# A fourth pair of chunks in the second feed-forward, with one split made by ScalarE and an on-chip transfer

## The chip, the cores and the metric

The kernel runs on one core of one Trainium2 chip. The core has a matrix engine (TensorE, PE in the profile; its weight loads are listed apart as PEld), VectorE (DVE), ScalarE (ACT), GpSimd (POOL) and a sync engine (SP), which run side by side, each through its own queue of instructions in a fixed order. They wait for each other by semaphores. Transfers between the chip's memory and the on-chip buffer are issued from the queues of SP, ACT or POOL and are carried out by the core's 16 DMA engines. The metric is the device time of one execution in microseconds (us), as the median of several runs.

## What is computed

One block of a streaming encoder for 256 tokens of width 1024: a gated feed-forward, a mixing stage with two attention-like branches, a cross-attention to a memory of 256 rows, and a second gated feed-forward. The change is made in the code of the feed-forwards:

```python
def rmsnorm(x, g):
    x32 = x.astype(jnp.float32)
    y = x32 * lax.rsqrt(jnp.mean(x32 * x32, axis=-1, keepdims=True) + EPS)
    return (y * g.astype(jnp.float32)).astype(x.dtype)

def swiglu(h, w_in, w_down):
    gate, up = jnp.split(h @ w_in, 2, axis=-1)
    return (jax.nn.silu(gate) * up) @ w_down
...
        h = rmsnorm(x, ffn2_pre_g[l])
        x = x + 0.5 * rmsnorm(swiglu(h, ffn2_w_in[l], ffn2_w_down[l]), ffn2_post_g[l])
```

`w_in` is 1024 x 5632 (gate and up), `w_down` is 2816 x 1024; all data are 32-bit floats.

## The kernel before

**Two halves of every number.** TensorE multiplies a shortened float format (fp32r in the profile). To keep the accuracy of 32-bit floats, every matrix is split into `hi`, the value rounded to that format, and `lo`, the remainder. A product is then three matmuls: hi by hi, hi by lo and lo by hi. For weights, each tile of 128 x 1024 numbers (512 KB) is loaded into a `raw` buffer, ScalarE casts it to `hi` (line 153 for plain weights, 173 for tiles of pairs) and VectorE subtracts `hi` from it to get `lo` (lines 155 and 174). There are 4 `raw` buffers, 8 `hi` and 8 `lo` buffers.

**The feed-forward** (function `ffn`). The 2816 hidden columns are cut into 11 chunks of 256, and each chunk has 256 gate columns and 256 up columns, four weight tiles in all. A plain chunk (`act_tok`) is computed for both halves of 128 tokens, 24 matmuls of 128 x 512 for each. Then silu(gate) times up (`act_evac`, lines 450 to 455) gives the chunk's activation `at`; four transposes on TensorE and a split (`flush`, line 445) turn it into the left operand `act` of the second matrix. A down step (`down`) multiplies the activation of one chunk and one half of the tokens with two tiles of `w_down`, 12 matmuls, and adds it up in PSUM (`acc`). The last three chunks' down steps (`STAG = 3`) are left for a tail, ordered by halves of the output columns, because the last norm (`post`) can begin on a half when it is complete.

**Pairs** (function `act_pair`). Two neighbouring chunks c and c+1 can be computed together by a scheme of Strassen and Winograd's kind: the two chunks, the two halves of the tokens and the two halves of the 1024 input rows form a 2 x 2 by 2 x 2 product of blocks, which needs 7 block products instead of 8. A block product is 12 matmuls (function `product`). With Bkn for rows' half k and chunk (n = 1 is c, n = 0 is c+1), the right operands are, in the order of the products:

1. `sums` = B00, into bank b1, saved by ScalarE (line 613)
2. `sums` + `both` (B01), into bank b4, saved (line 622)
3. that plus B11, added to b1, saved (line 627)
4. B11 itself, added to b4, which gives chunk c for the first tokens (line 634)
5. `both` + B11, added to b1, saved (line 637), which gives chunk c for the second tokens (line 640)
6. B10, into bank b0, which gives chunk c+1 for the first tokens (line 652)
7. the sum of all, added to b1, which gives chunk c+1 for the second tokens

The left operands are the matching sums of the input's blocks; they are made once (`pair_inputs`, lines 537 to 544). Each right operand is two tiles, so a pair splits 14 tiles. The sums of blocks are made in place by VectorE (`add`, line 592), 8 tiles a pair. Where a pair is listed in `FETCHED`, `both` + B11 is not added by VectorE but by a second, accumulating load of B11 from the chip's memory, issued from POOL (line 565); that is 2 adds fewer. `sums` and `both` of a pair live in four buffers (`extra`, named sraw in the profile), and the next pair's loads go into them when they are free (`pair_loads`, line 563).

Between the products, `step_between` puts half a down step of an earlier chunk (12 matmuls) onto TensorE, as many as there are in the list handed over; what is left follows after the seventh product.

Before, the second feed-forward takes chunks 0, 1, 2, 5 and 8 in the plain way and (3,4), (6,7), (9,10) as pairs, with 6, 6 and 2 halves of down steps inside the pairs, and nothing is fetched twice; the first feed-forward has the pairs (4,5), (6,7), (9,10), all in `FETCHED`.

**What sets the order.** Within an engine, instructions stay in a fixed order, which a planner makes when the kernel is built. It takes the instructions in the order of the program as their priority and lets a later one go ahead when its inputs and a buffer are ready earlier by the planner's own costs. `tc.high_priority()` and `tc.issue_after(...)` bend that order by hand. On the chip the order is kept, and an instruction that waits holds up all that stand behind it on its engine.

Of the kernel before, what the change touches and what calls it, by code (L numbers as in the profile page):

```python
# [11 lines left out]
F32 = mybir.dt.float32  # L12
# [20 lines left out]

STAG = 3

TOKS = {"f1_in": (3, 8), "f2_in": (2, 5, 8)}

PAIRS = {"f1_in": (4, 6, 9), "f2_in": (3, 6, 9)}

L_ACT = 21  # L40
L_F1 = 24
# [11 lines left out]
M_T = (106, 119)  # L53
M_O = (136, 140)

FETCHED = {"f1_in": (4,6,9), "f2_in": ()}
R_AT = (66, 130, 188, 252, 286, 332)

FG = 3
# [26 lines left out]
def block_kernel(ctx: ExitStack, tc: tile.TileContext, wts, head_in, gf_in, x_in, mem_in, memT_in, cols, rows, fbias, masks, out):  # L86
# [54 lines left out]
    def parts_of():  # L141
        return [wp.tile([P, D], F32R, tag=t, name=nm(t), bufs=8) for t in ("hi", "lo")]

    def load_split(src, n=512, behind=None, parts=None):

        raw = wp.tile([P, D], F32, tag="raw", name=nm("raw"), bufs=4)
        hi, lo = parts or parts_of()
        r, h, l = raw, hi, lo
        if n < 512:
            r, h, l = (p.rearrange("p (k n) -> p k n", k=2)[:, :, :n] for p in (raw, hi, lo))  # L150
        loads.append(nc.sync.dma_start(r, src).ins)
        with tc.issue_after(behind[0]) if behind else nullcontext():
            casts.append(S.copy(h, r).ins)  # L153
        with tc.issue_after(behind[1]) if behind else nullcontext():
            los.append(V.tensor_tensor(out=l, in0=r, in1=h.bitcast(F32), op=ALU.subtract).ins)  # L155
        return hi, lo

    def unit(name, i):
        u = _AT[name] + i
        if u not in cache:  # L160
            cache[u] = load_split(wts[u - 4], behind=hold.get(u), parts=place.get(u))
        return cache[u]

    def chunk(name, c):
# [4 lines left out]
        o = (kb % 2) * 512  # L169
        return hi[:, o : o + n], lo[:, o : o + n]  # L170

    def split(hi, lo, src):
        a = S.copy(hi, src)  # L173
        b = V.tensor_tensor(out=lo, in0=src, in1=hi.bitcast(F32), op=ALU.subtract)  # L174
        return a.ins, b.ins

# [250 lines left out]
    def ffn(w_in, w_dn, X, r2, n_tok, i_row, first_half, second_half=None):  # L427
# [132 lines left out]
        def more(r, c, k, n, j, op):  # L560
            src = wts[_AT[w_in] + 4 * (c + 1 - n) + 2 * k + j - 4]
            if op is None:
                loads.append(nc.sync.dma_start(r, src).ins)
            else:
                G.dma_start(r, src, accum_op=op)

        def act_pair(c, between):
            sx, q = pairs_in

            def of(n):  # L570
                return lambda kk: (sx[n][:, 0, kk], sx[n][:, 1, kk])

            def of_x(k):
                return lambda kk: (X.hi(4 * k + kk, 0, P), X.lo(4 * k + kk, 0, P))

            def splits(t):
                u = []
                for r in t:
                    p = parts_of()
                    split(p[0], p[1], r)  # L580
                    u.append(p)
                return u

            def raws(k, n):
                t = [wp.tile([P, D], F32, tag="raw", name=nm("raw"), bufs=4) for _ in range(2)]
                for j in range(2):
                    more(t[j], c, k, n, j, None)
                return t

            def add(t, o):  # L590
                for x, y in zip(t, o):
                    V.tensor_tensor(out=x, in0=x, in1=y, op=ALU.add)  # L592
# [12 lines left out]
            def half_tile(n):  # L605
                return sp.tile([P, 512], F32, tag="z2", name=nm(n), bufs=3)

            sums, both = sums_of_pair.pop(c)
            copies = [m4([P, 2, 512], n=n) for n in ("vw", "pc")]
            p1, v, w, p5 = (t[:, i] for t in copies for i in range(2))  # L610
            b1 = mm()
            product(b1, of_x(0), splits(sums), True)
            S.copy(p1, b1)
            add(sums, both)
            if c in FETCHED[w_in]:
                for j in range(2):
                    more(both[j], c, 1, 1, j, ALU.add)
            for _ in range(2 if c == 3 else 1):
                step_between()
            b4 = mm()  # L620
            product(b4, of("de"), splits(sums), True)
            S.copy(p5, b4)
            step_between()
            raw = raws(1, 1)
            add(sums, raw)
            product(b1, of("aed"), splits(sums), False)
            S.copy(v, b1)
            step_between()
            product(b4, of("baed"), splits(raw), False)
            if c not in FETCHED[w_in]:  # L630
                add(both, raw)
            with tc.high_priority():
                t = half_tile("c01")
                V.tensor_tensor(out=t, in0=b4, in1=v, op=ALU.subtract)
# [64 lines left out]
        for c in range(n_tok, NFF):  # L699
# [51 lines left out]
            while done < (NFF - STAG if last == NFF - 1 else min(c - 1 - (c + 1 in pairs), NFF - STAG - 1)):  # L751
# [856 lines left out]
```

## Time and profile before

| | |
|---|---|
| median of 3 runs | 772.19 us (772.18 to 773.46) |
| profiled execution | 772.46 us, of which 770.6 us are the span of the trace |
| PE busy | 762.0 us (99%) |
| VectorE busy | 635.2 us (82%) |
| ScalarE busy | 505.3 us (66%) |
| POOL busy | 20.4 us (3%) |
| DMA, hardware queue of SP | 144.83 MB, 53.9% of the 16 engines' span |
| DMA, POOL's queue | 4.60 MB, 3.1% |
| granted TensorE clock | 0.999 |

The profile is one execution. Busy times are sums over the span and hide that stages differ; a row of a stretch gives them for a part of it. Rows of groups have the form: line, engine, operation, what it writes and reads, shapes, count, then busy time and mean duration in ns, then idle time of the engine just before and who ended it. The chain of waits follows the last instruction back to what released it, step by step; what stands in it set the end, what doesn't was hidden. Rows of the timeline and of the chain begin with the start and the length in us. A matmul's row is longer than the distance to the next one, as they overlap; twelve in a row show the pace.

The second feed-forward begins at about 585 us; its first pair's inputs are made around 622 to 633 us, its pairs run until about 742 us, and its tail from there to 764 us.

### The profile page before, as it was taken

The numbers are of one execution on the slowest core, as the hardware profiler recorded it, in microseconds if no ns is written. First come the engines' busy times: TensorE is split into PE (matmuls) and PEld (weight loads), VectorE is DVE, ScalarE is ACT, GpSimd is POOL, SyncE is SP. The second block draws the span as 40 slices with busy tenths as digits, with TensorE's granted clock in tenths as the row PEclk, the third lists the DMA queues.
The fourth block names the chain that finished last, engine by engine and source line by source line (L and its number), as shares of the span: only waits on it lengthen the run. The fifth ranks groups of instructions, "written<-read, shape, count | busy, mean of one in ns | idle before, by whom it ended". The sixth has DMA issues, their size and how long they took to land.

```text
span 770.6 us, 11688 instructions
## 1 busy us (share of the span) xinstructions
PE 762.0 (99%) x4326; PEld 646.7 (84%) x4326; DVE 635.2 (82%) x939; ACT 505.3 (66%) x816; POOL 20.4 (3%) x42
## 2 busy tenths in 40 slices
PE   9999999999999999999999999999999999999996
PEld 8888788888888998898888888889888888888885
DVE  6799998998778898887776665885679899999973
ACT  8667576688774659667686345862668567775762
POOL 0000000000000100200000000000000000000000
PEclk9999999999999999999999999999999999999999
DMA  9768767674744545736476654466075616558331
GB/s 346 242 250 243 223 226 281 184 247 161 238 151 147 185 139 195 272 124 210 136 271 222 219 173 159 161 197 213 30 255 178 241 65 232 205 195 307 100 135 55
DMA packets 45129, 150.54 MB, mean 195 GB/s; under 512 B 5160, under 2 KB 8880, under 8 KB 45072
## 3 DMA queue, kind: packets, MB, share of 16 engines
q1 hardware_dynamic: 43168, 144.83, 53.9%
q0 software_dynamic: 1472, 4.60, 3.1%
q8 instruction: 34, 0.56, 0.3%
q10 hardware_dynamic: 432, 0.37, 0.1%
q14 instruction: 23, 0.19, 0.1%
HBM read 148.72 MB, written 1.06 MB: 194 GB/s over the span
## 4 chain that ended last, share of the span: by engine, by line
PE 90%; DVE 6%; DMA 2%; issue 1%; ACT 1%; DVEq 0%; ACTq 0%; SPq 0%
PE mm L100 46%; PE acc L100 36%; PE tr L100 5%; DVE sraw L592 1%; DVE lo L155 1%; DVE lo L174 1%; PE tr L445 1%; PE tr L385 1%; DMA sraw<-in_wts_dram 1%; DMA raw<-in_wts_dram 1%; DMA head<-in_head_dram 0%; DVE sx L174 0%; PE tr L1245 0%; ACT hi L153 0%; PE tr L1339 0%
## 5 line engine op out<-in xcount | busy, mean ns | idle before, releaser
L155 DVE TENSOR_TENSOR lo<-raw,hi 128x1024 fp32r<-128x1024 f32 (+1 forms) x204 | 241.3, 1200 | 37.5 <-ACT hi L153 30.9
L153 ACT CAST hi<-raw 128x1024 fp32r<-128x1024 f32 (+1 forms) x204 | 207.1, 1034 | 58.8 <-PE mm L100 30.4
L100 PE MATMUL mm<-hi,hlT 128*128 128x512 f32 (+1 forms) x688 | 209.4, 382 | 0.0
L100 PEld LDWEIGHTS mm<-hi,hlT 128*128 128x128 f32 x688 | 127.2, 188 | 22.3
L100 PE MATMUL mm<-lo,hlT 128*128 128x512 f32 (+1 forms) x344 | 130.1, 382 | 0.0
L100 PE MATMUL acc<-hi,act 128*128 128x512 f32 x352 | 113.6, 390 | 0.0
L173 ACT CAST hi<-sraw 128x1024 fp32r<-128x1024 f32 x60 | 62.6, 1052 | 25.5 <-DVE sraw L592 15.8
L100 PE MATMUL mm<-hi,sx 128*128 128x512 f32 x240 | 77.8, 390 | 0.0
L100 PEld LDWEIGHTS acc<-hi,act 128*128 128x128 f32 x352 | 66.1, 188 | 13.4
L100 PEld LDWEIGHTS mm<-lo,hlT 128*128 128x128 f32 x344 | 64.6, 188 | 10.8
L174 DVE TENSOR_TENSOR lo<-sraw,hi 128x1024 fp32r<-128x1024 f32 x60 | 72.1, 1220 | 0.8 <-ACT hi L173 0.5
L100 PE MATMUL acc<-lo,act 128*128 128x512 f32 x176 | 69.3, 394 | 0.0
L100 PE MATMUL acc<-hlT,hi 128*128 128x512 f32 x256 | 64.4, 393 | 0.0
L100 PEld LDWEIGHTS acc<-hlT,hi 128*128 128x128 f32 x256 | 46.1, 189 | 8.3
L100 PEld LDWEIGHTS mm<-hi,sx 128*128 128x128 f32 x240 | 44.9, 188 | 9.3
L100 PE MATMUL mm<-lo,sx 128*128 128x512 f32 x120 | 46.9, 391 | 0.1
L100 PEld LDWEIGHTS acc<-lo,act 128*128 128x128 f32 x176 | 33.1, 188 | 6.5
L100 PEld LDWEIGHTS acc<-hlT,lo 128*128 128x128 f32 x256 | 35.0, 190 | 2.5
L592 DVE TENSOR_TENSOR sraw<-sraw,raw 128x1024 f32<-128x1024 f32 x30 | 36.0, 1220 | 0.7 <-DMA raw<-in_wts_dram 0.6
L100 PE MATMUL acc<-hlT,lo 128*128 128x256 f32 x256 | 36.2, 283 | 0.0
L174 DVE TENSOR_TENSOR lo<-raw,hi 128x1024 fp32r<-128x1024 f32 x24 | 28.8, 1219 | 0.8 <-ACT hi L173 0.8
L100 PEld LDWEIGHTS mm<-lo,sx 128*128 128x128 f32 x120 | 22.5, 188 | 5.2 <-DVE lo L174 0.5
(285 smaller groups left out, 1192.4 us busy)
## 6 DMA issues: line engine op xcount, KB each, us to landing
raw<-in_wts_dram SPq DMA_DIRECT2D x223, 512.0 KB, 4.4
sraw<-in_wts_dram SPq DMA_DIRECT2D x24, 512.0 KB, 6.5
raw<-in_gf_dram SPq DMA_DIRECT2D x12, 344.0 KB, 3.8
sraw<-in_wts_dram POOLq DMA_DIRECT2D x6, 512.0 KB, 6.7
head<-in_head_dram SPq DMA_DIRECT2D x7, 392.0 KB, 6.3
grow<-in_rows_dram SPq DMA_DIRECT2D x4, 512.0 KB, 5.8
xs<-in_x_dram SPq DMA_DIRECT2D x2, 512.0 KB, 7.4
cb<-cd POOLq DMA_DIRECT2D x2, 512.0 KB, 6.1
```

Of the source, the lines that this page charges most:

```text
L100: log.append(PE.matmul(*args, **kw).ins)
L153: casts.append(S.copy(h, r).ins)
L155: los.append(V.tensor_tensor(out=l, in0=r, in1=h.bitcast(F32), op=ALU.subtract).ins)
L173: a = S.copy(hi, src)
L174: b = V.tensor_tensor(out=lo, in0=src, in1=hi.bitcast(F32), op=ALU.subtract)
L385: PE.transpose(blocks[-1][1], src(kb), ident)
L445: PE.transpose(trv[:, j, h * P : (h + 1) * P], ats[c, h][:, j * P : (j + 1) * P], ident)
L592: V.tensor_tensor(out=x, in0=x, in1=y, op=ALU.add)
```

## The change

- In the second feed-forward, chunks 5 and 8 are no longer plain: the pairs become (3,4), (5,6), (7,8), (9,10). The plain chunks are 0, 1 and 2.
- For the pairs 5, 7 and 9, `both` + B11 is made by the accumulating load (`FETCHED`), for pair 3 still by VectorE.
- For all four pairs, `lo` of B11 is made in another way (`BY_DMA`, `lo_by_dma`): ScalarE writes -1 times the raw tile, rounded to the format of `lo`, into `lo`, and a transfer from on-chip buffer to on-chip buffer, issued from POOL, adds the raw tile to it. `hi` is cast as before.
- In both feed-forwards, the two splits of B11 are called earlier: ahead of the sum for the third product instead of after the step that follows the third product.
- The down steps inside the second feed-forward's pairs are at most those of two chunks (4 halves): 0 and 1 in pair 3, 2 and 3 in pair 5, 4 and 5 in pair 7, 6 and 7 in pair 9. In the last pair, the step between the fifth and sixth product is left out, so its last half goes ahead of the seventh.
- Activations that have not been transposed by the end of the loop are flushed ahead of the tail.
- `TOTAL` is an option that is empty in both feed-forwards, and no B10 is in `BY_DMA`.

```diff
-TOKS = {"f1_in": (3, 8), "f2_in": (2, 5, 8)}
-
-PAIRS = {"f1_in": (4, 6, 9), "f2_in": (3, 6, 9)}
+TOKS = {"f1_in": (3,8), "f2_in": (2,)}
+
+PAIRS = {"f1_in": (4,6,9), "f2_in": (3, 5, 7, 9)}
...
-FETCHED = {"f1_in": (4,6,9), "f2_in": ()}
+TOTAL = {"f1_in": (), "f2_in": ()}
+FETCHED = {"f1_in": (4,6,9), "f2_in": (5, 7, 9)}
+
+BY_DMA = {("f2_in", c, "b11") for c in (3, 5, 7, 9)}
...
+    def lo_by_dma(l, r):
+        S.mul(l, r, -1.0)
+        G.dma_start(l.bitcast(F32), r, accum_op=ALU.add)
+
...
-    def split(hi, lo, src):
+    def split(hi, lo, src, by_dma=False):
         a = S.copy(hi, src)
+        if by_dma:
+            return lo_by_dma(lo, src)
         b = V.tensor_tensor(out=lo, in0=src, in1=hi.bitcast(F32), op=ALU.subtract)
...
             raw = raws(1, 1)
+            u11 = splits(raw, "b11")
             add(sums, raw)
             product(b1, of("aed"), splits(sums), False)
+            if c in TOTAL[w_in]:
+                for j in range(2):
+                    more(sums[j], c, 1, 0, j, ALU.add)
             S.copy(v, b1)
             step_between()
-            product(b4, of("baed"), splits(raw), False)
+            product(b4, of("baed"), u11, False)
...
-            step_between()
+            if c + 1 < NFF - 1 or first_half:
+                step_between()
             b0 = trp()
             raw = raws(1, 0)
             m = len(log)
-            product(b0, of_x(1), splits(raw), True)
+            product(b0, of_x(1), splits(raw, "b10"), True)
             if late[:1] == [c]:
                 flush(m + 10)
-            add(sums, raw)
+            if c not in TOTAL[w_in]:
+                add(sums, raw)
...
-                downs = [(i, h) for i in range(done, min(c, NFF - STAG - 1)) for h in range(2)]
-                done = max(done, min(c, NFF - STAG - 1))
+                upto = max(done, min(c, NFF - STAG - 1) if first_half else min(c, done + 2, NFF - STAG))
+                downs = [(i, h) for i in range(done, upto) for h in range(2)]
+                done = upto
...
+        while late:
+            flush(len(log))
         left, right = (0, 512), (512, 1024)
```

More of the change, by code (lines that the diff above doesn't have):

```diff
@@ L142, in parts_of, with load_split @@
         return [wp.tile([P, D], F32R, tag=t, name=nm(t), bufs=8) for t in ("hi", "lo")]
-    def load_split(src, n=512, behind=None, parts=None):
+    def lo_by_dma(l, r):
+        S.mul(l, r, -1.0)
+        G.dma_start(l.bitcast(F32), r, accum_op=ALU.add)
+    def load_split(src, n=512, behind=None, parts=None, by_dma=False):
         raw = wp.tile([P, D], F32, tag="raw", name=nm("raw"), bufs=4)
@@ L153, in load_split @@
             casts.append(S.copy(h, r).ins)
+        if by_dma:
+            lo_by_dma(l, r)
+            return hi, lo
         with tc.issue_after(behind[1]) if behind else nullcontext():
@@ L160, in unit @@
         if u not in cache:
-            cache[u] = load_split(wts[u - 4], behind=hold.get(u), parts=place.get(u))
+            cache[u] = load_split(wts[u - 4], behind=hold.get(u), parts=place.get(u), by_dma=(name, i) in BY_DMA)
         return cache[u]
@@ L170, in blk @@
         return hi[:, o : o + n], lo[:, o : o + n]
-    def split(hi, lo, src):
+    def split(hi, lo, src, by_dma=False):
         a = S.copy(hi, src)
+        if by_dma:
+            return lo_by_dma(lo, src)
         b = V.tensor_tensor(out=lo, in0=src, in1=hi.bitcast(F32), op=ALU.subtract)
@@ L574, in of_x, with splits @@
                 return lambda kk: (X.hi(4 * k + kk, 0, P), X.lo(4 * k + kk, 0, P))
-            def splits(t):
+            def splits(t, of=None):
                 u = []
@@ L579, in splits @@
                     p = parts_of()
-                    split(p[0], p[1], r)
+                    split(p[0], p[1], r, (w_in, c, of) in BY_DMA)
                     u.append(p)
```

## The prediction

> **What bounds the kernel now.** I read the page first, then the busy times by stretch, then the chain of waits, then the groups and single rows of the second feed-forward. The page says that TensorE is busy all the time and carries nine tenths of the chain.
>
> ```profile
> span 770.6 us, 11688 instructions
> ...
> PE 762.0 (99%) x4326; PEld 646.7 (84%) x4326; DVE 635.2 (82%) x939; ACT 505.3 (66%) x816; POOL 20.4 (3%) x42
> ...
> PE 90%; DVE 6%; DMA 2%; issue 1%; ACT 1%; DVEq 0%; ACTq 0%; SPq 0%
> ```
>
> Those shares are means over unlike stages. The stretches tell more (columns: length, then busy time of PE, PEld, DVE, ACT, POOL, then granted clock, DMA share, GB/s). The first runs from the first down step inside the first pair of the second feed-forward to the start of its tail, the second covers the three pairs of the first feed-forward.
>
> ```profile
> 622.70:747.70 125.00, 124.84 (x566) 102.53 (x565) 121.24 (x131) 86.38 (x108) 0.00 (x0) 1.00 0.54 190
> ...
> 40.00:165.00 125.00, 124.05 (x565) 102.16 (x564) 119.45 (x131) 87.23 (x111) 5.24 (x6) 1.00 0.71 231
> ```
>
> In the stretch that the change rewrites, PE idles 0.16 us of 125, at full clock; VectorE works 121.24 us and so has only 3.76 us to spare. Both are at their limit. The chain shows how close the second one is:
>
> ```profile
> 612.37 4.22 DMA raw<-in_wts_dram
> ...
> 633.50 1.06 ACT hi L173
> ...
> 655.76 2.35 DVE lo L155 x2
> 658.12 0.41 DVE at L455
> ...
> 658.57 0.44 PE tr L445 x2
> 659.01 12.28 PE mm L100 x54
> 671.28 2.72 PE acc L100 x12
> ...
> 685.38 5.44 PE mm L100 x24
> ...
> 741.71 2.75 PE acc L100 x12
> 744.45 0.43 PE tr L445 x4
> 744.89 19.08 PE acc L100 x84
> ```
>
> Up to 658.57 us the chain runs through VectorE (the `lo` and `at` rows): in the first pair, VectorE sets the pace. From there to 763.97 it is TensorE alone. Twelve matmuls, which are one product or one half of a down step, take 2.72 us; two `lo` in a row take 2.35 us, so one takes 1.13 us of VectorE when they follow each other.
>
> **The change part by part.**
>
> *Fourth pair.* Chunks 5 and 8 leave the plain path and the pairs become (3,4), (5,6), (7,8), (9,10). Two plain chunks are 96 matmuls, a pair is 7 x 12 = 84. The down steps, their weights and the transposes stay the same in number. So PE loses 12 matmuls: -2.72 us, and since PE idles only 0.16 us in the stretch, this is on the path.
>
> *VectorE's bill.* These groups are those of the stretch 622.7 to 747.7, the last one ScalarE's of 598.6 to 750:
>
> ```profile
> L155 DVE TENSOR_TENSOR lo<-raw,hi 128x1024 fp32r<-128x1024 f32 x27 | 32.3, 1220 | 1.7 <-ACT hi L153 1.6
> ...
> L592 DVE TENSOR_TENSOR sraw<-sraw,raw 128x1024 f32<-128x1024 f32 x16 | 19.3, 1219 | 0.0
> L174 DVE TENSOR_TENSOR lo<-raw,hi 128x1024 fp32r<-128x1024 f32 x12 | 14.4, 1218 | 0.0
> ...
> L634 DVE TENSOR_TENSOR c<-mm,vw 128x512 f32<-128x512 f32 x3 | 2.1, 685 | 0.0
> ...
> L173 ACT CAST hi<-raw 128x1024 fp32r<-128x1024 f32 x12 | 12.4, 1050 | 1.9 <-DMA raw<-in_wts_dram 0.9 <-ACT hi L153 0.7 <-ACT hi L173 0.4
> ```
>
> Before, the pairs and plain chunks 5 and 8 need 3 x 14 + 8 = 50 `lo`; after, 4 x 14 less the 8 of B11 make 48. Adds: 3 x 8 = 24 before; after 8 in pair 3 and 6 in the three pairs whose `both` is fetched, 26. These cancel. The fourth pair adds three combining subtractions or additions (lines 634, 640, 652), 3 x 0.6 = 1.8 us. So VectorE needs 121.24 + 1.8 = 123.0 us, and PE leaves it 125.0 - 2.72 = 122.3 us: the by-transfer `lo` and the fetched sums do not relieve VectorE, they only pay for the fourth pair. There is one cushion. VectorE's last piece, the `lo` of the last activation, ends at 747.7 (the row of 747.01 below) while its down step comes after twelve matmuls of the tail. The last 84 matmuls are one half step of chunk 7 and the tail's six groups, so the tail starts at 744.89 + 2.7 = 747.6 and that step at 750.3. That leaves 2.6 us: VectorE has 122.3 + 2.6 = 124.9 us for 123.0 us of work and may idle 1.9 us before PE pays. It idled 3.76 us before. If it idles as much again, 1.9 us of the gain are given back; if it idles little, because a queue that is behind does not wait, nothing. I take 0.7, nearer to nothing: 1.7 us of the idle time stand in the L155 row, as waits for casts of plain chunks and down weights, and the plain chunks go. Ends: 0 and 1.9.
>
> *ScalarE.* 6 more casts (56 against 42 + 8) and 8 multiplications by -1, which the trace doesn't show; by the cast of the same shape 1.05 us each. 14 x 1.05 = 14.7 us on 86.38 of 122.3 us: hidden, if the order on its queue is good.
>
> *B11's lo by transfer.* The new chain is cast, multiplication, issue on POOL, accumulating transfer. The nearest rows are the first feed-forward's accumulating loads:
>
> ```profile
> L565 POOL DMA_DIRECT2D sraw<-in_wts_dram x6: 853/868/916, 54.9 to 133.7; - x6
> ...
> DMA to landing us min/median/max: 5.1/6.7/8.3
> ```
>
> From the start of the cast to the landing: 1.05 + 1.05 + 0.87 + 6.7 = 9.7 us (8.1 to 11.3). The second tile's casts come 2.1 us later, and its first use is six matmuls (1.36 us) later. What is available is seen from when B11 is cast now and when its product starts (pair 3, 6 and 9; the product of pair 6 is the chain's 685.38):
>
> ```profile
> 634.46 2.00 ACT L173 CAST hi<-raw 128x1024 fp32r<-128x1024 f32 x2
> 675.44 1.06 ACT L173 CAST hi<-raw 128x1024 fp32r<-128x1024 f32 x1 [0.69 <-ACT hi L153]
> 720.73 2.00 ACT L173 CAST hi<-raw 128x1024 fp32r<-128x1024 f32 x2
> ...
> 639.95 0.39 PE L100 MATMUL mm<-hi,sx 128*128 128x512 f32 x1
> ...
> 727.58 8.18 PE mm L100 x36
> ```
>
> 5.5 us, 9.9 us and 9.6 us (730.3 - 720.7). With the old order pair 3 would come 4.2 us late. But the change calls this split ahead of the sum for the product before it, and the raw tile of pair 3 has landed by 616.6 (the chain's 612.37 + 4.22), so it can start as soon as the first product gives its buffers back, six steps of 2.72 us (16 us) ahead of the fourth product. In the later pairs it is five steps, 13.6 us. I take no stall; ends 0 and 4.2 us a pair. Queued behind on POOL is only the other tile's transfer and the fetched `both`, whose product is one step later.
>
> The Trainium skill, page "DMA: Bandwidth & Descriptors", section "Anatomy of one DMA — SWDGE (gpsimd) path", gives 2.0 us plus bytes over 436 KB per us for such a transfer, an estimate of 3.2 us for 512 KB. By it the chain from the cast would be about 6.2 us, the forecast the same 770.2 us and the late transfer no rival in pairs 6 and 9; the row of 6.7 us is of the same kind of transfer and decides.
>
> *Pairs without a plain chunk between.* The next pair's tiles can only be loaded when this pair's last split has freed theirs. The first feed-forward has one such place (pair 4 to 6), on the chain:
>
> ```profile
> 84.46 5.61 DMA sraw<-in_wts_dram
> ...
> 90.16 1.23 DVE sraw L592
> 91.39 1.14 DVE lo L155
> 92.52 0.41 DVE at L455
> ...
> 92.97 0.44 PE tr L445 x2
> ```
>
> The load is released late, the add waits for it at the head of VectorE's queue, `at` waits behind, and PE waits about 1 us. After the change there are three such places, with no down step after the last product; but each pair has 2 x 1.13 us less to do on VectorE than that one. I count the wait into the 0.7 above; ends 0 and 3 x 1 = 3 us.
>
> *Tail and flush.* The last pair now uses its four down steps inside (one is skipped), so nothing covers the last activation but the tail's first twelve matmuls.
>
> ```profile
> 742.91 0.46 ACT L450 ACTIVATE sg<-mm,facs 128x256 f32<-128x256 f32 x1
> ...
> 744.80 1.04 ACT L153 CAST hi<-raw 128x1024 fp32r<-128x1024 f32 x1
> ...
> 747.01 0.68 DVE L174 TENSOR_TENSOR act<-tr,act 128x512 fp32r<-128x512 f32 x1
> ```
>
> From the silu's start to the end of the activation's `lo` 4.8 us pass now, with a down weight's cast of 1.04 us within; twelve matmuls and four transposes are 2.72 + 0.43 = 3.1 us. Ends 0 and 1.7 us; I take 0, as that cast can come earlier when the down steps do, and matmuls of the other half of the columns are ready to fill the hole.
>
> *First feed-forward.* B11's split moves ahead there too, with `lo` still on VectorE: 2.3 us more before the third product's `lo`. In pair 6 these end at 101.5 and the product starts at 104.8, a lead of 3.3 us, so it is covered. Ends -1 (the wait above goes by chance of the new order) and +1 us.
>
> ```profile
> 99.17 2.36 DVE L174 TENSOR_TENSOR lo<-sraw,hi 128x1024 fp32r<-128x1024 f32 x2
> ...
> 104.78 2.72 PE mm L100 x12
> ```
>
> Sum: -2.72 + 0.7 = -2.0 us on the profiled execution of 772.46 us (span 770.6 and 1.9 around it). That execution lies 0.27 us above the median of the runs, so 772.19 - 2.0 = 770.2 us.
>
> **The rivals.**
>
> *Given back, no change.* VectorE idles as before, or the three joints cost 1 us each: 772.2 - 2.7 + 1.9 to 3.0 = 771.4 to 772.5 us. For it: VectorE's 123.0 against 122.3 us. Against it: the second half of the stretch is PE alone on the chain.
>
> *Slower: B11's lo lands late.* Place: the fourth product of each pair. It decides from 2.72 / 4 = 0.7 us a pair on. If the casts stay where they stand now, pair 3 costs 4.2 us and the others about 0.3 each: +2.4, 774.6 us; with 2 us in each pair +5.3, 777.5 us. For it: queue orders are fixed ahead and pair 6 has no slack at all. Against it: the new place of the split.
>
> *The transfers crowd the loads.* Eight transfers on chip and six fetched sums are 14 x 0.52 = 7.3 MB.
>
> ```profile
> q0 software_dynamic: 1472, 4.60, 3.1%
> ```
>
> At this queue's rate (3.1% of 770.6 us for 4.6 MB, 5.2 us a MB) they take 38 us, and the DMA share goes from 0.54 to (67.5 + 38) / 122.3 = 0.86. The first feed-forward runs at 0.71 with the 1 us above. If a load lands 1.5 us later at each of three joints, and PE pays that beside the 1 us, 3 x 2.5 = 7.5: +4.8, 777.0 us. The page "DMA: Bandwidth & Descriptors" of the Trainium skill says under "Issuing engines are not separate DMA queues" that all issuers share the same 16 engines, which is the mechanism of this rival; the shares here fit it.
>
> **How the numbers follow.** Forecast (give-back under 1.2 us): 0.45, with its own range 769.0 to 770.7. Given back: 0.30. Late lo: 0.17. Crowded loads: 0.08. A measurement of this kernel tells about 0.2%, 1.5 us, from no change; so faster 0.45, same 0.30, slower 0.25. Low end: the full 2.72, PE's 0.16 us of idle time in the stretch and a third of the first feed-forward's possible 1 us, 769.0. High end: into the late-lo case, past 774.6, to 775.0, which leaves out about 0.1 above.
>
> **What would show it.** Right: PE's busy time in the stretch about 2.7 us shorter, 12 matmuls fewer, VectorE near 100% busy from 620 to 745, the tail's row unchanged, POOL with eight more transfers landing in 5 to 8 us before the fourth product. Wrong: waits of PE on an accumulating transfer (late lo), on `at` or on sraw loads at 650, 680 and 710 (joints), landing times of loads up (crowding), or new gaps between 55 and 165 us (first feed-forward).

## The result, and the profile after

The changed kernel takes 778.75 us (median of 4 runs, 778.34 to 779.33) against 772.18 us before: a ratio of 1.0082 (95% interval 1.0064 to 1.0099). It is slower by 6.6 us, where 770.2 us and a range up to 775.0 us were forecast. The profiled execution of the changed kernel is one of 779.33 us, with a span of 777.5 us. Its page:

```profile
span 777.5 us, 11754 instructions
...
PE 761.3 (98%) x4314; PEld 645.3 (83%) x4314; DVE 636.5 (82%) x942; ACT 518.5 (67%) x834; POOL 33.7 (4%) x56
...
q1 hardware_dynamic: 43168, 144.83, 53.4%
q0 software_dynamic: 3488, 11.94, 7.9%
...
PE 71%; DVE 12%; DMA 9%; issue 5%; ACT 2%; POOL 0%; SPq 0%; DVEq 0%; ACTq 0%; POOLq 0%
```

The twelve matmuls are gone (4314 against 4326), but only 71% of the chain is TensorE's (90% before), and 9% is now DMA. The stretches say where; the columns are as in the prediction, the first row is of the kernel before, the two below of the changed one:

```profile
622.00:750.00 128.00, 127.84 (x580) 105.02 (x580) 121.94 (x132) 86.38 (x108) 0.00 (x0) 1.00 0.53 185
```

```profile
622.00:750.00 128.00, 119.35 (x532) 97.21 (x531) 116.94 (x126) 94.50 (x119) 12.20 (x14) 0.99 0.81 240
...
40.00:165.00 125.00, 124.89 (x568) 102.88 (x567) 120.29 (x133) 87.36 (x112) 5.19 (x6) 1.00 0.73 235
```

The first feed-forward has gained (TensorE idles 0.11 us of 125 instead of 0.95). In the pairs of the second one TensorE idles 8.65 us of 128, and VectorE, which the prediction put at its limit, idles 11 us. Both wait for something else. TensorE's waits from 600 us on:

```profile
PE tr L457 <- DVE at L467: 5.1, 2, 2.8
PE tr L457 <- DVE at L465: 3.2, 1, 3.2
```

These are three waits of 2.8, 2.3 and 3.2 us, each at the transposes of an activation (line 457, `flush`) in the midst of the sixth product, in the pairs 5, 7 and 9: 8.3 us. VectorE delivers `at` late. What made VectorE late in the pair 5 is read backwards, from VectorE's rows to ScalarE's to the loads (SP) and the transfers (the chain):

```profile
669.09 1.23 DVE L186 TENSOR_TENSOR lo<-raw,hi 128x1024 fp32r<-128x1024 f32 x1 [1.94 <-ACT hi L183]
672.59 1.23 DVE L186 TENSOR_TENSOR lo<-raw,hi 128x1024 fp32r<-128x1024 f32 x1 [2.27 <-ACT hi L183]
...
680.94 0.48 DVE L467 SCALAR_TENSOR_TENSOR at<-c,q,sg 128x256 f32<-128x256 f32 x1
```

```profile
668.01 1.05 ACT L183 CAST hi<-raw 128x1024 fp32r<-128x1024 f32 x1 [2.27 <-DMA raw<-in_wts_dram]
671.51 1.05 ACT L183 CAST hi<-raw 128x1024 fp32r<-128x1024 f32 x1 [2.45 <-DMA raw<-in_wts_dram]
```

```profile
663.75 2.81 SPq L575 DMA_DIRECT2D raw<-in_wts_dram  x2
```

```profile
656.11 0.09 POOL lo L149
656.19 1.09 issue
657.28 8.83 DMA lo<-raw
...
666.23 5.20 DMA raw<-in_wts_dram
671.43 0.02 issue
...
671.51 1.06 ACT hi L183
...
672.59 1.23 DVE lo L186
```

B10, the operand of the sixth product, is loaded late: its second load is issued at 666.2, the moment the on-chip transfer of B11's second tile lands, because that transfer reads the `raw` buffer which B10's load wants. It lands at 671.4. VectorE, with B10's two `lo` ahead of everything else in its fixed order, stands still for 1.94 and 2.27 us and starts `at` at 680.94. And the transfer itself took 8.8 us. The stretches show the engines of the DMA at that time (columns as above, the last two are DMA share and GB/s; the first is when the two fetches of `both` run, the second when the two transfers on chip run, the third has plain loads only):

```profile
651.00:656.50 5.50, 5.50 (x25) 4.53 (x25) 5.50 (x8) 5.50 (x8) 1.27 (x2) 1.00 0.99 186
660.00:664.50 4.50, 4.50 (x24) 3.70 (x22) 4.29 (x5) 4.50 (x6) 0.00 (x0) 1.00 1.07 221
672.00:674.00 2.00, 2.00 (x10) 1.67 (x9) 1.41 (x2) 0.56 (x1) 0.00 (x0) 1.00 1.01 401
```

All 16 engines are busy in all three, but the accumulating transfers move 186 and 221 KB per us (GB/s in the rows) and the plain loads 401. A pair with fetches and transfers on chip so keeps the engines busy for some 10 us with 2 MB, and all that comes in between waits: two loads of down weights, issued at 654, move from 657 to 661, and the transfers on chip, issued at 656.1 and 657.3, move from 660 on.

Two ways are left in which this makes B10 late. **Hold**: the transfer keeps the raw buffer until it lands, so the load is issued late. **Queue**: the packets of plain loads stand behind the accumulating ones, so the transfers and the loads themselves take longer. The experiments are to tell them apart, and both from the prediction's bound, **VectorE's amount of work**.

### The profile page after: what moved, and what is told of

The parts are those of the page before. It is cut to its first block, busy times and chain, and to the rows that moved or that the text cites. A ratio compares the mean times of both kernels' runs of the same rounds, so it can differ in the third digit from the quotient of the medians.

```text
span 777.5 us, 11754 instructions
## 1 busy us (share of the span) xinstructions
PE 761.3 (98%) x4314; PEld 645.3 (83%) x4314; DVE 636.5 (82%) x942; ACT 518.5 (67%) x834; POOL 33.7 (4%) x56
## 3 DMA queue, kind: packets, MB, share of 16 engines
q1 hardware_dynamic: 43168, 144.83, 53.4%
## 4 chain that ended last, share of the span: by engine, by line
PE 71%; DVE 12%; DMA 9%; issue 5%; ACT 2%; POOL 0%; SPq 0%; DVEq 0%; ACTq 0%; POOLq 0%
PE mm L103 34%; PE acc L103 31%; PE tr L103 4%; DVE lo L186 4%; DVE sraw L604 4%; DMA raw<-in_wts_dram 3%; DMA sraw<-in_wts_dram 3%; DMA lo<-raw 2%; DVE lo L165 2%; ACT hi L183 1%; PE tr L397 1%; DVE sx L186 1%; PE tr L457 0%; ACT hi L160 0%; DVE at L465 0%
## 5 line engine op out<-in xcount | busy, mean ns | idle before, releaser
L165 DVE TENSOR_TENSOR lo<-raw,hi 128x1024 fp32r<-128x1024 f32 (+1 forms) x196 | 231.7, 1198 | 34.9 <-ACT hi L160 28.8
L160 ACT CAST hi<-raw 128x1024 fp32r<-128x1024 f32 (+1 forms) x196 | 198.4, 1032 | 51.4 <-PE mm L103 30.3
L103 PE MATMUL mm<-hi,hlT 128*128 128x512 f32 (+1 forms) x632 | 192.0, 382 | 0.0
L103 PEld LDWEIGHTS mm<-hi,hlT 128*128 128x128 f32 x632 | 116.6, 188 | 20.1
L103 PE MATMUL mm<-lo,hlT 128*128 128x512 f32 (+1 forms) x316 | 119.2, 381 | 0.0
L183 ACT CAST hi<-sraw 128x1024 fp32r<-128x1024 f32 x70 | 72.5, 1051 | 44.9 <-DVE sraw L604 37.1
L103 PE MATMUL mm<-hi,sx 128*128 128x512 f32 x280 | 91.7, 393 | 0.2 <-DVE sx L186 0.2
L186 DVE TENSOR_TENSOR lo<-sraw,hi 128x1024 fp32r<-128x1024 f32 x70 | 83.6, 1217 | 0.7 <-ACT hi L183 0.4
L103 PE MATMUL mm<-lo,sx 128*128 128x512 f32 x140 | 55.1, 394 | 0.0
L183 ACT CAST hi<-raw 128x1024 fp32r<-128x1024 f32 x28 | 29.0, 1051 | 12.6 <-DMA raw<-in_wts_dram 12.2
```

The lines of the kernel that those rows point to most:

```text
L103: log.append(PE.matmul(*args, **kw).ins)
```

## The experiments

All against the kernel before, run on the same chip in turn. The table has them together; work is VectorE's busy time over the whole kernel by each page (before 635.2, changed kernel 636.5 us).

| run | pairs with fetch | tiles by transfer | work | median us | ratio to before |
|---|---|---|---|---|---|
| changed kernel | 5, 7, 9 | 8 | 636.5 | 778.75 | 1.0082 [1.0064, 1.0099] |
| e1, only B11 earlier | none | 0 | 635.0 | 772.37 | 0.9987 [0.9978, 0.9996] |
| e2, tiles of their own | 5, 7, 9 | 8 | 638.3 | 806.48 | 1.0421 [1.0404, 1.0439] |
| e3, no transfers | 5, 7, 9 | 0 | 645.7 | 774.91 | 1.0021 [1.0012, 1.0030] |
| e4, no fetches | none | 8 | 642.6 | 771.06 | 0.9970 [0.9958, 0.9982] |
| e5, plain fetches | 5, 7, 9 | 8 | 636.9 | 772.78 | 1.0006 [0.9994, 1.0017] |
| e6, plain copies | 5, 7, 9 | 8 | 636.3 | 772.86 | 1.0007 [0.9992, 1.0021] |
| e7, source hi | 5, 7, 9 | 8 | 636.5 | 780.24 | 1.0099 [1.0084, 1.0114] |
| e8, transfers in pair 3 | 5, 7, 9 | 2 | 643.2 | 771.26 | 0.9978 [0.9969, 0.9988] |
| e9, half the transfers | 5, 7, 9 | 5 | 639.6 | 772.89 | 1.0005 [0.9996, 1.0015] |
| e10, half the fetches | 5, 7, 9 | 8 | 639.5 | 773.94 | 1.0021 [1.0011, 1.0031] |
| e11, lo on POOL | 5, 7, 9 | 0 | 653.3 | 785.63 | 1.0164 [1.0149, 1.0179] |
| e12, pairs alone | none | 0 | 651.9 | 781.86 | 1.0118 [1.0104, 1.0131] |
| e13, bound, raw | 5, 7, 9 | 8 | 637.1 | 783.84 | 1.0128 [1.0106, 1.0150] |
| e14, bound, hi | 5, 7, 9 | 8 | 637.3 | 777.74 | 1.0064 [1.0043, 1.0085] |

### e1: only the earlier call, in the kernel before

```diff
             raw = raws(1, 1)
+            u11 = splits(raw)
             add(sums, raw)
...
-            product(b4, of("baed"), splits(raw), False)
+            product(b4, of("baed"), u11, False)
```

> The kernel before with nothing but the earlier call of B11's split, in both feed-forwards, lo still on VectorE. In the changed kernel the wait of TensorE at the joint of pairs 4 and 6 of the first feed-forward shrank from 1.22 to 0.38 us and everything behind it came 1.0 us earlier. If that is the earlier call alone: 771.2 us (-1.0), from the first feed-forward, nothing from the second. Rival, the 1.0 us came from the rest of the change through the planner's order: 772.2 us.

The kernel before took 773.33 us on this chip, e1 772.37, a gain of 1.0 us (0.3 to 1.7). Its row of the first feed-forward:

```profile
40.00:165.00 125.00, 125.00 (x569) 103.19 (x568) 120.01 (x131) 87.60 (x113) 5.23 (x6) 1.00 0.73 232
```

TensorE's 0.95 us of idle time are gone: the gain of the first feed-forward belongs to the earlier call alone. In the profiled execution 0.8 us come back as a wait in the first pair of the second feed-forward, so how much of the 1.0 us stays there isn't settled.

### e2: B11's raw tiles in tiles of their own

```diff
+                own = (w_in, c, "b11") in BY_DMA and n == 1
-                t = [wp.tile([P, D], F32, tag="raw", ...) for _ in range(2)]
+                t = [m4([P, D], n="own") if own else wp.tile([P, D], F32, tag="raw", ...) for _ in range(2)]
```

> The changed kernel, but B11's raw tiles of the second feed-forward lie in two tiles of their own and not in two of the four raw buffers. Transfers, multiplications, VectorE's work and DMA bytes are the same. Theory (the on-chip transfer reads B11's raw buffer until it lands, and SP's next load, B10's, waits for that buffer; then B10's hi, VectorE's lo and the at behind it come late): the three waits of TensorE in the sixth product (2.9, 2.4 and 3.4 us, and about 1 us of slow matmuls behind the first) go, 769 to 771 us. Rival, crowding of the DMA engines: loads land as late as now, 777 to 779 us. Rival, VectorE has too much to do for a fourth pair: at stays late, 776 to 779 us.

It took 806.48 us and answers nothing: the new tiles come from the pool of activations and inputs, the planner makes another order of it, and TensorE waits 21.2 us for casts and 5.3 us for the transfers themselves. The hold has to be taken away without another order (e7, e14).

### e3 and e4: one of the two parts removed

```diff
-BY_DMA = {("f2_in", c, "b11") for c in (3, 5, 7, 9)}
+BY_DMA = set()
```

> The changed kernel with B11's lo on VectorE in all pairs: no multiplications by -1, no transfers on chip; the four pairs and the fetched sums stay. VectorE has 8 lo more, 9.0 us. Theory of the held buffer: B10's load is early again and VectorE's idle time of about 10 us (waits of its lo for ScalarE's hi) is filled by the 9 us of work; by the prediction's bill 123.0 + 9.0 against 124.9 us, 7.1 us too much: about 776 to 778 us, with waits of TensorE on at and lo spread over the pairs and no wait of VectorE on a late B10. Rival, crowding by the transfers on chip is all there is: 772 to 774 us.

```diff
-FETCHED = {"f1_in": (4,6,9), "f2_in": (5, 7, 9)}
+FETCHED = {"f1_in": (4,6,9), "f2_in": ()}
```

> The changed kernel with both + B11 added by VectorE in all four pairs: six accumulating loads (3.1 MB) fewer, six adds (7 us) more on VectorE; the transfers on chip stay. Theory of the held buffer: the late B10 stays, VectorE has 7 us more behind it; 780 to 786 us. Rival, the fetched sums crowd the loads: B10 lands earlier, 775 to 778 us.

Without transfers (e3) 774.91 us, 1.6 us slower than before; without fetches (e4) 771.06 us, 2.3 us faster than before. Both expectations of the held buffer alone fell: taking the fetches away, with 6.1 us more work for VectorE, made the kernel 8.6 us faster than the changed one, by the ratios. In e4 B10's loads of the pair 5 are issued 1.3 us earlier, its two casts run one behind the other with no wait, and VectorE is full (in e3 it works 126.9 of the same 128 us, and TensorE waits 2.6 us for ScalarE's casts). The rows of e4:

```profile
662.48 2.27 SPq L575 DMA_DIRECT2D raw<-in_wts_dram  x2
```

```profile
668.26 1.99 ACT L183 CAST hi<-raw 128x1024 fp32r<-128x1024 f32 x2
```

```profile
622.00:750.00 128.00, 126.90 (x573) 103.43 (x573) 127.26 (x139) 98.92 (x124) 6.96 (x8) 1.00 0.72 218
```

The transfers of this pair are issued within 0.5 us of each other in the two kernels, and without fetches ahead of them they land after 5.7 and 7.2 us instead of 7.5 and 8.8. The down weights' two loads that SP issues at 654 land after 3.2 and 4.4 us instead of 6.2 and 6.4.

### e5 and e6: the same instructions in the same order, plain packets

```diff
-                G.dma_start(r, src, accum_op=op)
+                G.dma_start(r, src, **({} if w_in == "f2_in" else {"accum_op": op}))
```

> The changed kernel, but in the second feed-forward the six fetches of B11 overwrite both and don't add to it (both + B11 becomes B11: the sum is left out). Instructions, their order on every engine and the bytes are the same; only the packets of six transfers change from accumulating to plain. Reason: in the changed kernel, from 651 to 657 us the two accumulating fetches of a pair keep the engines busy at 190 KB per us, half of what plain loads move behind them, and two weight loads and then the on-chip transfers are served behind. If the queue of the engines makes B10 late, plain fetches bring the on-chip transfers to their end about 2 us earlier and B10 too: waits of TensorE of 3 us become about 1 us, 772 to 775 us. If only the hold of the raw buffer by its own transfer counts: 777 to 779 us.

```diff
-        G.dma_start(l.bitcast(F32), r, accum_op=ALU.add)
+        G.dma_start(l.bitcast(F32), r)
```

> The changed kernel, but the transfers on chip of B11's lo copy and don't add (lo becomes the raw tile: the subtraction is left out). Instructions and their order are the same on every engine. The transfers' share of the engines halves (2.6 us less a pair by the pace of plain loads), the raw buffers come free some 3 us earlier, B10 loads earlier by as much: by both theories (held buffer, queue of the engines) the three waits go nearly, 770 to 773 us. If VectorE's amount of work made at late, with 123.0 us unchanged: 777 to 779 us.

772.78 us (e5) and 772.86 us (e6): by the ratios, each takes 6 us off the changed kernel, and nothing else is altered than whether six or eight transfers accumulate. Bytes, instructions and order are the same on every engine; POOL's issue of a plain transfer is 0.3 us shorter. In the pair 5 the transfers on chip land after 6.2 and 7.8 us in e5, after 6.0 and 6.3 us in e6, and after 7.5 and 8.8 us in the changed kernel. The transfers on chip as plain copies, in e6:

```profile
660.00:662.00 2.00, 2.00 (x13) 1.67 (x11) 1.79 (x3) 2.00 (x3) 0.00 (x0) 1.00 1.04 424
```

424 KB per us instead of 221 for the same two tiles. With that the waits of TensorE for `at` fall from 8.3 to 2.7 us (e6), and to 3.2 us in e5, whose profiled execution of 774.53 us lies 1.8 us above its median:

```profile
PE tr L457 <- DVE at L467: 1.7, 2, 1.3
PE tr L457 <- DVE at L465: 1.0, 1, 1.0
```

```profile
PE tr L457 <- DVE at L467: 3.2, 2, 2.6
```

VectorE's work is that of the changed kernel in both, so its amount isn't what costs the 6.6 us. The fetches do not touch the raw buffers; that plain fetches help as much as plain copies shows the queue at the engines: the transfers behind them land earlier.

### e7, e13 and e14: the hold taken away

```diff
-    def lo_by_dma(l, r):
+    def lo_by_dma(l, r, h=None):
...
-        G.dma_start(l.bitcast(F32), r, accum_op=ALU.add)
+        G.dma_start(l.bitcast(F32), h.bitcast(F32), accum_op=ALU.add)
...
-            return lo_by_dma(lo, src)
+            return lo_by_dma(lo, src, hi)
```

> The changed kernel, but the accumulating transfer reads B11's hi tile and not its raw tile (lo becomes zero: the remainder is left out). Packets, bytes, VectorE's work and SP's order are the same, so are all orders up to the second pair; but the raw buffers are free when VectorE's add has read them (about 658 and 659 us in the second pair, against 663.7 and 666.2). Theory of the held buffer: B10's loads are issued 5 to 7 us earlier, hi and lo of B10 come in time, 770 to 773 us. Rival, it is the queue of the engines alone: B10's packets stand behind the transfers' all the same and land as now, 777 to 779 us.

780.24 us, a little above what the queue alone would give, but the run doesn't show that. In the pair 5, where the order is the same, B10's loads went out at 658.7 and 659.9 and landed only 9.1 and 9.8 us later, the second 1.7 us earlier than in the changed kernel, and TensorE's wait fell from 2.8 to 0.5 us by its rows. In the pair 7 the planner, which now counts on an earlier B10, had put the add of B10 ahead of a down weight's `lo`, and VectorE stands there:

```profile
691.12 1.45 SPq L575 DMA_DIRECT2D raw<-in_wts_dram  x2
```

```profile
700.14 1.22 DVE L604 TENSOR_TENSOR sraw<-sraw,raw 128x1024 f32<-128x1024 f32 x1 [5.56 <-DMA raw<-in_wts_dram]
```

So both sources were run again (e13 with raw, e14 with hi) with the add bound behind B10's `lo`, which makes the order on every engine the same in these two:

```diff
-                    split(p[0], p[1], r, (w_in, c, of) in BY_DMA)
+                    last_lo[:] = [split(p[0], p[1], r, (w_in, c, of) in BY_DMA)]
...
-            if c not in TOTAL[w_in]:
+            with nullcontext() if first_half else tc.issue_after(last_lo[0][1]):
                 add(sums, raw)
```

> The changed kernel, with the add of B10 to the sums bound behind B10's second lo on VectorE in the second feed-forward (the order differs from the changed kernel by a few neighbours changing places). Control for the next run: 778 to 780 us, with waits of about 3 us in the sixth product of three pairs.

> As the control, order the same on every engine, but the accumulating transfer on chip reads hi and not raw (lo becomes zero: the remainder is left out), so that the raw buffers are free some 5 us earlier. If the hold of the raw buffer makes B10 late: 770 to 772 us. If the queue at the DMA engines makes it late: 777 to 779 us. By the second pair of the run with hi as source, where B10's second tile landed 1.7 us earlier and the wait of TensorE fell from 3.0 to 0.8 us: both count, hold 2 us a pair, 772 to 774 us.

783.84 us with raw as source (the control, above the 778 to 780 expected), 777.74 us with hi: the hold is worth about 5 us in this order by the ratios, 6 by the medians. TensorE's waits, e13 first:

```profile
PE tr L457 <- DVE at L467: 5.5, 2, 3.5
PE tr L457 <- DVE at L465: 5.2, 1, 5.2
```

```profile
PE tr L457 <- DVE at L465: 3.8, 1, 3.8
PE tr L457 <- DVE at L467: 1.8, 3, 1.4
```

And ScalarE's casts of B10 in the pair 5, with its wait for the load, e13 first:

```profile
667.99 1.05 ACT L183 CAST hi<-raw 128x1024 fp32r<-128x1024 f32 x1 [1.64 <-DMA raw<-in_wts_dram]
671.19 1.05 ACT L183 CAST hi<-raw 128x1024 fp32r<-128x1024 f32 x1 [2.15 <-DMA raw<-in_wts_dram]
```

```profile
667.56 1.05 ACT L183 CAST hi<-raw 128x1024 fp32r<-128x1024 f32 x1 [1.83 <-DMA raw<-in_wts_dram]
668.85 1.06 ACT L183 CAST hi<-raw 128x1024 fp32r<-128x1024 f32 x1 [0.23 <-DMA raw<-in_wts_dram]
```

The two loads of B10 themselves, e13 first:

```profile
664.20 2.83 SPq L575 DMA_DIRECT2D raw<-in_wts_dram  x2
```

```profile
658.31 1.96 SPq L575 DMA_DIRECT2D raw<-in_wts_dram  x2
```

In e14 they go out at 658.3 and 659.4 (664.2 and 666.7 in e13), 6 to 7 us earlier, but land after 9.2 and 9.3 us instead of 3.7 and 4.4. For the first tile the queue takes all of what the hold took, its cast waits as before; the second tile's cast comes 2.3 us earlier, of which 0.6 us are e14's lead at the beginning of this stretch (its transfers are issued 0.6 us earlier), and its wait is nearly gone. The totals of e13 and e14 are to be read against each other: 777.7 us lies in the band given for the queue alone, but that band counted on a control of 778 to 780 us. Why the control itself is some 4 us slower than the changed kernel isn't shown. Over the kernel before, 0.6% (0.4 to 0.9) are left with the hold gone, and with the clash gone (e4, e8) none. So both count, one behind the other: accumulating fetches delay the transfers, the transfers hold the buffers longer, and B10's loads go out late or stand in the queue.

### e8, e9 and e10: less of the clash

e8 has the transfers in pair 3 alone, where nothing is fetched:

```diff
-BY_DMA = {("f2_in", c, "b11") for c in (3, 5, 7, 9)}
+BY_DMA = {("f2_in", c, "b11") for c in (3,)}
```

> The changed kernel with transfers on chip in the first pair alone; the fetches stay in the other three, so that no pair has both. VectorE has six lo more (6.8 us), as much as without the fetches. If the clash of fetch and transfer within a pair is the cause of the loss: as without the fetches, 770.5 to 772 us. If the loss without transfers (774.9 us) comes from the last three pairs and not from the first: 774 to 775 us.

771.26 us, as expected: fetches in three pairs and transfers in the fourth, with nothing of both in one pair, give the same as transfers in all four and no fetches. TensorE and VectorE are both near full:

```profile
622.00:750.00 128.00, 127.17 (x572) 102.83 (x571) 126.97 (x138) 92.54 (x118) 7.00 (x8) 1.00 0.73 218
```

Then half of a clash, in the pairs 5, 7 and 9 (e9 one tile by transfer, e10 one tile fetched):

```diff
-                for r in t:
+                for j, r in enumerate(t):
...
-                    split(p[0], p[1], r, (w_in, c, of) in BY_DMA)
+                    split(p[0], p[1], r, (w_in, c, of) in BY_DMA and (c == 3 or j == 1))
```

> The changed kernel, but in the second, third and fourth pair only the second of B11's two tiles gets its lo by transfer, the first on VectorE (three lo, 3.4 us, more for VectorE); the first pair has both transfers, the fetches stay. Accumulating transfers of such a pair keep the engines busy for three times 2.6 us and not four. Theory of the queue at the engines: as with plain copies or plain fetches, which took the same 2.6 us a pair away (772.8 us), but without their remainder of waits in the third pair if the first tile's raw buffer comes free early: 770.5 to 772.5 us. Rival, one transfer behind two fetches is enough to make B10 late: 774 to 777 us.

```diff
-                for j in range(2):
+                for j in range(2 if first_half else 1):
                     more(both[j], c, 1, 1, j, ALU.add)
...
             if c not in FETCHED[w_in]:
                 add(both, raw)
+            elif not first_half:
+                add(both[1:], raw[1:])
```

> The changed kernel, but in the second, third and fourth pair only the first of both's two tiles is fetched, the second is added by VectorE (three adds, 3.4 us, more); all transfers on chip stay. Again 2.6 us less of the engines a pair. Theory of the queue at the engines: 770.5 to 772.5 us. Rival, the transfers on chip make B10 late by themselves as soon as VectorE has more to do: 774 to 777 us.

772.89 us (e9), between the two bands expected, and 773.94 us (e10), at the lower edge of the rival's. Both are slower than e4 and e8 although VectorE has 3 us less work than there. In e10 TensorE still waits 2.4 us for `at`. In e9 the waits have another place (TensorE for the `lo` of a down weight, 1.4 us). Which part of this is half a clash at the engines and which the planner's other order isn't shown.

### e11: lo on POOL

```diff
         if by_dma:
-            return lo_by_dma(lo, src)
+            return G.tensor_tensor(out=lo, in0=src, in1=hi.bitcast(F32), op=ALU.subtract)
```

> The changed kernel, but B11's lo is subtracted by POOL, from raw and hi, and not made by a multiplication and a transfer: no transfers on chip, 8 us less for ScalarE, VectorE's work as in the changed kernel. No row shows POOL subtracting 128 x 1024 numbers. If it takes up to 5 us a tile and VectorE keeps its 1.2 us a tile: 769 to 770.5 us, the time that was forecast. Rival, VectorE slows down while POOL works, or POOL takes over 6 us a tile, so that lo lands after the fourth product's turn: 774 to 785 us.

785.63 us: the rival. POOL's row of the pair 5, and VectorE's meanwhile:

```profile
658.41 11.40 POOL L185 TENSOR_TENSOR lo<-raw,hi 128x1024 fp32r<-128x1024 f32 x2 [0.93 <-ACT hi L183]
```

```profile
664.26 6.63 DVE L186 TENSOR_TENSOR lo<-sraw,hi 128x1024 fp32r<-128x1024 f32 x2
```

POOL takes 5.7 us a tile here, and two `lo` of VectorE take 6.63 us instead of 2.35. Just before, also beside POOL, two other `lo` of VectorE and two adds each took the usual 2.35 us. Over the kernel VectorE's busy time grows by 16.8 us (653.3 against 636.5) for the same 942 instructions. The page "SBUF — State Buffer" of the Trainium skill, section "Who interferes with whom", says that a VectorE instruction with two inputs in the on-chip buffer contends with a POOL instruction that reads there; these rows agree.

### e12: four pairs alone

```diff
-FETCHED = {"f1_in": (4,6,9), "f2_in": (5, 7, 9)}
+FETCHED = {"f1_in": (4,6,9), "f2_in": ()}
...
-BY_DMA = {("f2_in", c, "b11") for c in (3, 5, 7, 9)}
+BY_DMA = set()
```

> Four pairs in the second feed-forward with neither fetches nor transfers: VectorE makes all lo and all sums, 14 tiles more than in the changed kernel. By the prediction's bill (123.0 + 14 x 1.13 = 138.8 us against 124.9 us) 13.9 us too much: 768.5 + 13.9 = 782 us. By what six adds more really cost VectorE (642.6 - 636.5 = 6.1 us) and how little TensorE paid for them (771.1 us without fetches), 776 to 779 us. If VectorE were no bound: 769 us.

781.86 us, the 782 of the prediction's bill. VectorE has 15.4 us more work than in the changed kernel (651.9 against 636.5, 1.10 us a tile), and

```profile
622.00:750.00 128.00, 120.86 (x532) 95.62 (x531) 125.45 (x134) 82.08 (x104) 0.00 (x0) 1.00 0.50 170
```

TensorE idles 7 us with VectorE at 98%. So VectorE is the bound of four pairs that have neither relief, and something has to be taken off it: by the ratios, transfers alone (e4) take 11.4 us off this kernel, fetches alone (e3) 7.5 us, and both together (the changed kernel) only 2.8 us. The two reliefs do not add up.

## Why the prediction was wrong, step by step

- **Fourth pair**, -2.72 us: the 12 matmuls went, as said. The gain is seen only where nothing waits: e4 and e8 are 2.3 and 1.7 us faster than before, of which up to 1.0 us is the first feed-forward's.
- **VectorE's bill**, 123.0 us against 122.3, cushion 1.9: right as a count of work. With the 14 tiles put back the time is that of the bill (e12). But in the changed kernel VectorE idles 11 of 128 us, and the bill did not bind. That the changed kernel gives 0.7 us back on this account can't be read from it. The exact agreement of e12 is luck in part: six tiles more cost less than the bill (6.8 us by it, 4.9 us past its cushion, and e4 is still at 771.1), and the other eight cost more (11.4 us from e4 to e12, 9.0 by the bill).
- **ScalarE**, 14.7 us hidden: right. Its busy time grew by 13.2 us, and it waits for loads, not the other way round.
- **B11's lo by transfer**: this is the step that failed. It was put at 0 us; in its place came three waits, 8.3 us by their rows. Its sum, 9.7 us from cast to landing for the first tile and 11.8 us for the second, came out as 11.2 and 13.7 us (casts from 652.36 on, landings at 663.6 and 666.1). It also counts POOL's 0.87 us twice, as the time to landing begins with POOL's row (657.28 and 8.83 us are 666.11, and the load into the freed buffer goes out at 666.23). "I take no stall" held at the place the step looked at: the fourth product of the pair 5 starts at 667.7 us, 1.6 us behind the last landing, and waits for nothing. The late-lo rival was wrong. What the step left out is what the transfer does to others: it reads the raw buffer until it lands, and SP's next load stands behind it. The step looked at what is queued behind on POOL and not at who waits for the tile that is read. Between e13 and e14 this is worth 5 to 6 us.
- **The transfers crowd the loads**, given 0.08 and 777.0 us: this lengthens the hold, and e5 and e6 show that without it nearly all of the loss is gone. Its volume was right (DMA share 0.86 foreseen, 0.81 found). Its chance was put too low because 0.86 was read as a mean. The mean hides a burst: from 651 to 665 us the engines are full or nearly so, most of that time at half the pace, and B10's load comes at its end. The half pace stood in the page of before, and the step used it for its mean: 4.60 MB in 3.1% of the span is 5.2 us a MB, 144.83 MB in 53.9% is 2.9 us a MB. The place was wrong, the sixth product and not the joints, so that the price of three times 2.5 us came near the measured one by luck.
- **What the prediction drew on beside the rows**: by the page "DMA: Bandwidth & Descriptors" of the Trainium skill, section "Anatomy of one DMA — SWDGE (gpsimd) path", 512 KB would take an estimated 3.2 us; the accumulating transfers on chip landed after 6.5 to 8.8 us, and the measurement decides. The same page of the Trainium skill, section "Issuing engines are not separate DMA queues", says that transfers of all issuers run on the same 16 engines. The runs agree: two loads from SP's queue land 2 to 3 us later behind fetches from POOL's (e4 against the changed kernel).
- **Pairs without a plain chunk between**, counted into 0.7: right, TensorE doesn't wait at the joints. VectorE waits for a sum's load twice from 600 us on, 0.7 us in all (0.48 us at 683.0).
- **Tail and flush**, 0 taken: right, no wait of TensorE behind 750 us.
- **First feed-forward**, 0 taken, ends -1 and +1: the end of -1 came, 0.95 us by the row of e1.

The sum as it came: -2.7 (matmuls) - 1.0 (first feed-forward) + 8.3 (three waits) + 1.2 (half clock behind the first wait, below) = +5.8 us. The two profiled executions differ by 6.9 us. Of the remaining 1.1 us, 0.5 belong to the waits too: counted from the start of one row to the next, and less what the same steps take elsewhere, they cost 8.8 us. The rest lies in small gaps.

What stays open: how hold and queue share the loss in the changed kernel's own order. The 5 to 6 us between e13 and e14 are of an order that is itself 4 us slower.

e4 beats both kernels, by 0.3% the one before (0.18 to 0.42%): four pairs, all of B11's lo by transfer and nothing fetched.

## What to carry to other kernels

A transfer that relieves an engine has two prices beside its own latency: it keeps the buffer it reads until it lands, and it takes its turn in DMA engines that all queues share. Cost both at the place where the next load wants that buffer, and look at bursts rather than the mean share. Accumulating transfers count about twice their bytes (here 186 and 221 KB per us against 401 and 424), and two reliefs that each pay alone can cost more than both bring when they fall into the same 15 us.

## What the runs showed of the hardware beside this

- The 16 engines move accumulating packets at about half the pace of plain ones: 186 (from memory) and 221 KB per us (on chip) against 401 and 424.
- POOL is busy 0.87 us for issuing an accumulating transfer of 512 KB and 0.55 us for a plain one of the same shape (e5, e6).
- During TensorE's pause of 2.8 us at 678.7 the granted clock fell to 0.50, at about 680.8, and stayed there until about 684.2. TensorE worked at this clock for 2.7 us, and matmuls came 0.43 us apart instead of 0.23:

```profile
682.30:684.10 1.80, 1.80 (x6) 1.32 (x4) 1.32 (x2) 0.67 (x2) 0.00 (x0) 0.50 0.98 398
```

  The page "TensorE: Matmul & The Clock Gate" of the Trainium skill, section "What's actually happening", has the clock halved after an idle window of about 3.4 us that runs freely. The time at half clock agrees with that size, 3.4 us; the pause was shorter here, and behind the longer one at 744 us, of 3.2 us, the clock stayed at 1.00.
- POOL subtracted two tiles of 128 x 1024 numbers in 5.2 to 11.4 us, and beside the longest of these two `lo` of VectorE took 6.63 us instead of 2.35 (e11).
